# A two-layer decoder trunk: the second feed-forward matrix by seven products, product sums in PSUM, and a new weight ring

## Chip, cores and metric

One core of a Trainium2 chip runs the whole kernel in one launch. The metric is device time in microseconds, from start to end of an execution. The engines are named as in the profile: PE (TensorE, matrix products), DVE (VectorE), ACT (ScalarE), POOL (GpSimd), SP (SyncE, which here issues the DMAs).

## What is computed

Two decoder layers on 512 tokens of width 1024, in float32. Layer 0 mixes tokens by differential and block-sparse attention, layer 1 by gated linear attention; the change does not touch them. After each mixer comes the feed-forward part, which it does touch:

```python
def sqrelu_mlp(x, w1, w2):          # x: 512x1024, w1: 1024x4096, w2: 4096x1024
    return jnp.square(jax.nn.relu(x @ w1)) @ w2

for l in range(DEPTH):              # DEPTH = 2
    ...
    x = layer_norm(DEEPNORM_ALPHA * x + mix, ln_mix_g[l], ln_mix_b[l])
    x = layer_norm(DEEPNORM_ALPHA * x + sqrelu_mlp(x, ffn_w1[l], ffn_w2[l]), ln_ffn_g[l], ln_ffn_b[l])
```

## The kernel before

**Precision by three products.** Each float32 operand is split into a high part in the format fp32r (a copy on ACT) and a low part (a subtraction on DVE); for a weight `parts` does both (L110, L111). A product is then three matmuls into one PSUM bank, high x high, high x low, low x high (`mm3`, L171 to L173).

**Weights** come as units of 512 KB in the order of their use, on SP's queue (L92), into four raw buffers (`rp`). `pump` splits the next unit where the count of units ahead is under a cap; `nxt` takes a unit, `free` gives its buffer back.

**The feed-forward part** (`ffn`) walks through the 4096 hidden features in four blocks of 8 x 128. In a block it first makes hidden features with the first matrix, `pa` banks or pairs, then multiplies them with the block's rows of the second matrix, `pf` banks, and adds the results into `x` (`resid`, L296 and L298).

*First matrix.* A unit is 1024 inputs x 128 hidden features: 8 x 3 = 24 matmuls of 128x512, a plain unit. Two units together can instead go as a pair by the Winograd form of a 2x2 block product, 7 products in place of 8, each of 4 x 3 matmuls of 128x256: 84 matmuls of 256 columns in place of 48 of 512. Its right operands are sums of token quarters, made once per layer (`right_operands`). Its weight sums are made and split by `split_pair` (L135 to L139, then L110 and L111), and `pair` makes the four results out of seven products, each in its own half of a bank `pp`: ACT copies one (p1, L772), DVE adds the rest (L767). Then come relu (L787), square (L712) and the split of the hidden features (L714, L715). Six plain units stand at the head of block 0; the other 26 units of a layer are 13 pairs.

*Second matrix.* Always plain: two halves of 512 output columns, each 8 hidden chunks x 4 token tiles x 3 matmuls of 128x512, so 192 per block, into four banks that DVE adds into `x` after each half.

**Order.** The code names instructions in program order; a scheduler places them on each engine by its own estimates and by urgency marks, so a queue's order is not the text's. Each engine then works strictly in its queue's order.

Of the kernel before, what the change touches and what calls it, by code (L numbers as in the profile page):

```python
# [46 lines left out]
def trunk(ctx, tc, a, out):  # L47
# [34 lines left out]
    NU = wst.shape[0]  # L82
    raws, units, late = {}, {}, {}
    W = {"dma": 0, "split": 0, "used": 0, "slots": 0, "cap": 6}
    pairs = {u + 16 * b + j for u in FFN_UNITS for b in range(FF // P // FBLK) for j in range(0 if b else NPLAIN, FBLK, 2)}

    def dma_unit():
        for fn in late.pop(W["dma"], ()):
            fn()
        if W["dma"] < NU:  # L90
            r = rp.tile([P, 1024], F32, tag="raw", name="raw")
            nc.sync.dma_start(r, wst[W["dma"]])  # L92
            raws[W["dma"]] = r
            W["dma"] += 1

    def pop_raw():
        u = W["split"]
        while W["dma"] <= u:
            dma_unit()
        W["split"] += 1  # L100
        return raws.pop(u)

    def ahead():
        while W["dma"] < min(W["split"] + 4, NU):
            dma_unit()

    def parts(w, i, src):

        n = src.shape[-1] // 512
        A.activation(w[:, 0, i:i + n, :], src.rearrange("p (n c) -> p n c", n=n), AF.Copy)  # L110
        V.tensor_tensor(w[:, 1, i:i + n, :], src.rearrange("p (n c) -> p n c", n=n), w[:, 0, i:i + n, :].bitcast(F32),  # L111
                        op=ALU.subtract)
# [1084 lines left out]
```

## Time and profile before

| | before |
|---|---|
| time, median of 3 runs | 1173.81 us (1173.73 to 1173.92) |
| profiled execution, its own time | 1172.42 us |
| its span (first to last instruction) | 1170.6 us |
| PE busy | 1155.2 us, 99 % of the span |
| DVE busy | 793.0 us, 68 % |
| ACT busy | 548.1 us, 47 % |
| first layer's feed-forward part | about 254.8 to 597.5 us |
| second layer's feed-forward part | about 832 to 1164.5 us |

An engine's busy time is the union of its instructions' durations, so a PE whose matmuls overlap can be busy all the time; what a matmul costs is read from the distance of two starts. Idle time in brackets stands before the row's first instruction, with what ended it.

### The profile page before, as it was taken

What the parts mean: (1) busy time and instruction counts of PE and PEld (TensorE: products, weight loads), DVE (VectorE), ACT (ScalarE), POOL (GpSimd) and SP (SyncE); (2) the same over time, 40 slices, a digit from 0 to 9 for tenths busy, and PEclk for the clock granted to TensorE, in tenths of its full rate; (3) what the DMA queues carried; (4) which work ended last, traced back from release to release, by engine and by line L of the source; (5) the groups of instructions that cost most, each with busy time, mean ns of one, the idle gap of its engine ahead of it and who ended that gap; (6) DMA issues with size and microseconds to landing.
All of it is one profiled execution on the core that took longest, in us unless ns stands there. A gap on an engine that the chain in (4) does not pass through costs nothing.

```text
span 1170.6 us, 16693 instructions
## 1 busy us (share of the span) xinstructions
PE 1155.2 (99%) x6682; PEld 1008.9 (86%) x6682; DVE 793.0 (68%) x1299; ACT 548.1 (47%) x890; POOL 48.4 (4%) x64
## 2 busy tenths in 40 slices
PE   9999999999999999999999999999999999999997
PEld 6788877898899899899888888888988998988986
DVE  6788673679468477487547656587784874865946
ACT  5745375547237146156236433643471551642631
POOL 1122300000000000000110000000000000000000
PEclk9999999999999999999999999999999999999999
DMA  9622050023226125127123122501051251251421
GB/s 319 232 72 73 8 161 32 19 73 118 99 60 191 38 73 180 54 67 252 37 68 108 55 72 73 180 19 57 34 181 54 70 165 55 87 165 36 121 78 73
DMA packets 34094, 114.33 MB, mean 98 GB/s; under 512 B 4192, under 2 KB 5216, under 8 KB 34016
## 3 DMA queue, kind: packets, MB, share of 16 engines
q1 hardware_dynamic: 32368, 108.22, 28.6%
q0 software_dynamic: 1648, 5.05, 1.4%
q8 instruction: 52, 0.85, 0.3%
q14 instruction: 26, 0.21, 0.1%
HBM read 111.15 MB, written 2.10 MB: 97 GB/s over the span
## 4 chain that ended last, share of the span: by engine, by line
PE 93%; issue 2%; ACT 2%; DVE 1%; DMA 0%; POOL 0%; DVEq 0%; ACTq 0%; POOLq 0%
PE pf L171 11%; PE pf L172 11%; PE pf L173 11%; PE pp L173 7%; PE pp L172 7%; PE pp L171 7%; PE pa L171 5%; PE pa L173 5%; PE pa L172 5%; PE pb L171 3%; PE pb L172 3%; PE pb L173 3%; PE pl L1000 2%; PE sc L521 1%; PE pv L171 1%
## 5 line engine op out<-in xcount | busy, mean ns | idle before, releaser
L111 DVE TENSOR_TENSOR w<-raw,w 128x1024 fp32r<-128x1024 f32 (+1 forms) x190 | 222.2, 1179 | 57.2 <-ACT w L110 56.3
L110 ACT ACTIVATE w<-raw 128x1024 fp32r<-128x1024 f32 (+1 forms) x190 | 188.2, 997 | 92.2 <-DMA raw<-in_wst 19.9
L171 PE MATMUL pf<-w,hh 128*128 128x512 f32 x504 | 196.4, 390 | 0.0
L172 PE MATMUL pf<-w,hh 128*128 128x512 f32 x504 | 196.2, 389 | 0.0
L173 PE MATMUL pf<-w,hl 128*128 128x512 f32 x504 | 196.1, 389 | 0.0
L110 ACT ACTIVATE w<-sf 128x1024 fp32r<-128x1024 f32 x52 | 55.0, 1058 | 215.6 <-PE pf L173 138.7
L172 PE MATMUL pp<-xTl,w 128*128 128x256 f32 x416 | 117.7, 283 | 0.0
L173 PE MATMUL pp<-xTh,w 128*128 128x256 f32 x416 | 117.7, 283 | 0.0
L171 PE MATMUL pp<-xTh,w 128*128 128x256 f32 x416 | 117.7, 283 | 0.0
L173 PEld LDWEIGHTS pf<-w,hl 128*128 128x128 f32 x504 | 94.6, 188 | 19.8
L171 PEld LDWEIGHTS pf<-w,hh 128*128 128x128 f32 x504 | 94.6, 188 | 19.5
L172 PEld LDWEIGHTS pf<-w,hh 128*128 128x128 f32 x504 | 94.6, 188 | 19.1
L171 PE MATMUL pa<-xTh,w 128*128 128x512 f32 x264 | 106.0, 403 | 0.0
L173 PE MATMUL pa<-xTh,w 128*128 128x512 f32 x264 | 103.1, 391 | 0.0
L172 PE MATMUL pa<-xTl,w 128*128 128x512 f32 x264 | 102.9, 390 | 0.0
L111 DVE TENSOR_TENSOR w<-sf,w 128x1024 fp32r<-128x1024 f32 x52 | 63.6, 1224 | 56.5 <-ACT w L110 56.5
L171 PE MATMUL pp<-T,w 128*128 128x256 f32 x312 | 88.3, 283 | 0.0
L172 PE MATMUL pp<-T,w 128*128 128x256 f32 x312 | 88.3, 283 | 0.0
L173 PE MATMUL pp<-T,w 128*128 128x256 f32 x312 | 88.3, 283 | 0.0
L171 PEld LDWEIGHTS pp<-xTh,w 128*128 128x128 f32 x416 | 79.8, 192 | 0.3
L172 PEld LDWEIGHTS pp<-xTl,w 128*128 128x128 f32 x416 | 79.8, 192 | 0.3
L173 PEld LDWEIGHTS pp<-xTh,w 128*128 128x128 f32 x416 | 79.8, 192 | 0.0
(260 smaller groups left out, 2264.2 us busy)
## 6 DMA issues: line engine op xcount, KB each, us to landing
raw<-in_wst SPq DMA_DIRECT2D x190, 512.0 KB, 3.8
xraw<-in_xT SPq DMA_DIRECT2D x8, 256.0 KB, 5.1
x<-in_x SPq DMA_DIRECT2D x4, 512.0 KB, 6.9
gb<-in_lng POOLq DMA_DIRECT2D x4, 512.0 KB, 5.7
gb<-in_lnb POOLq DMA_DIRECT2D x4, 512.0 KB, 7.5
out_x<-x SPq DMA_DIRECT2D x7, 256.0 KB, 2.0
tab<-in_rope SPq DMA_DIRECT2D x2, 512.0 KB, 5.9
raw<-in_wst SPq DMA_DIRECT2D x4, 128.0 KB, 4.4
```

The lines of the kernel that those rows point to most:

```text
L110: A.activation(w[:, 0, i:i + n, :], src.rearrange("p (n c) -> p n c", n=n), AF.Copy)
L111: V.tensor_tensor(w[:, 1, i:i + n, :], src.rearrange("p (n c) -> p n c", n=n), w[:, 0, i:i + n, :].bitcast(F32), op=ALU.subtract)
L171: PE.matmul(o, l[0], r[0], start=first, stop=False)
L172: PE.matmul(o, l[0], r[1], start=False, stop=False)
L173: PE.matmul(o, l[1], r[0], start=False, stop=last)
L521: PE.matmul(ps[:, :n], q, k, start=i == 0, stop=False)
L1000: PE.matmul(pl[:, h * P:(h + 1) * P], z, z, start=True, stop=True)
```

## The change

- **Second matrix.** In blocks 0, 1 and 2 of each layer `second` makes the product by 7 products of half size, each 2 x 2 x 2 x 3 = 24 matmuls of 128x512. Left operands are sums of hidden-feature quarters (`s1`, the in-place sums of `a21` and `a12`, then the split by `left` into tiles `ho`); right operands are sums of weight quarters made in place in four tiles `w2` (`add_block`, L230) and split into the ring. Products that enter one result in sequence accumulate in one pair of banks, and are added into `x` after each step: 14 residual adds in place of 8. Block 3 stays plain.
- **First matrix.** `PLAIN = (6, 4, 4, 0)` plain units by block: 1, 2, 2 and 4 pairs, 9 per layer for 13. In `pair` four products accumulate in the bank `ba` and two in `bc`; ACT copies their content in between (p1 L878, u2 L886; p5 L882), DVE's adds read it (L805).
- **Weights.** The ring `qp` has 7 half buffers of 1024 values per partition. A plain unit or an entry of the second matrix takes 2, an entry of a pair 2 or 1 (7 for the whole pair). A plain unit can also take a whole buffer of pool `u`, up to `W["un"]`, which is 0 in the feed-forward part but for its end. Three raw buffers in place of four; pools are opened anew by stage.

The core of the diff; in the new kernel line numbers are other ones, and L117 is the low part of any split, L116 its high part, L867 a pair's matmul, L394 and L396 residual adds.

```diff
-NPLAIN = 6
+NB = FF // P // FBLK
+PLAIN = (6, 4, 4, 0)
+NQ = 7
...
-    rp = ctx.enter_context(tc.tile_pool(name="rp", bufs=4))
+    rp = ctx.enter_context(tc.tile_pool(name="rp", bufs=3))
+    qp = ctx.enter_context(tc.tile_pool(name="qp", bufs=NQ))
...
+    def room(kind):
+        if kind == "unit":
+            return W["q"] + 2 <= NQ or W["u"] < W["un"]
+        return W["q"] + kind <= NQ
+
+    def take(kind):
+
+        if kind == "unit" and W["q"] + 2 > NQ:
+            W["u"] += 1
+            w = t8("w", (P, 2, 1024), F32R)
+            return ("u", 1), w[:, 0], w[:, 1]
+        n = 1 if kind == 1 else 2
+        W["q"] += n
+        if n == 1:
+            w = q4()
+            return ("q", 1), w[:, :512], w[:, 512:]
+        return ("q", 2), q4(), q4()
+
...
+        steps = ((0, 0, None), (0, 0, lambda a, b_, c, d: sub(a, b_, a)), (0, 0, lambda a, b_, c, d: sub(a, d, a)),
+                 (1, 0, None), (0, 1, lambda a, b_, c, d: sub(b_, d, b_)), (1, 1, None),
+                 (1, 0, lambda a, b_, c, d: sub(c, c, a)))
+        return [entry(i, n, half, pre, m == 6) for m, (i, n, pre) in enumerate(steps) for half in range(2)]
...
+        def pair(p, right):
+
+            ba, bb, bc = (bank("pp")[:, :256] for _ in range(3))
...
+            p1, p5, u2 = t1("p1"), t1("p5"), t1("u2")
+            c11, c12, c21, c22 = H[0][:, 0, p, :], H[0][:, 1, p, :], H[1][:, 0, p, :], H[1][:, 1, p, :]
+            w = nxt()
+            prod(ba, w, 0, "b11", True)
+            A.activation(p1, ba, AF.Copy)
+            v = nxt()
+            prod(bc, v, 0, "t1", True)
+            done(v)
+            A.activation(p5, bc, AF.Copy)
+            v = nxt()
+            prod(ba, v, 0, "t2", False)
+            done(v)
+            A.activation(u2, ba, AF.Copy)
+            prod(bb, w, 1, "b21", True)
+            done(w)
+            add(c11, p1, bb)
+            w = nxt()
+            prod(ba, w, 0, "t3", False)
+            add(c22, p5, ba)
+            v = nxt()
+            prod(bc, v, 0, "b22", False)
+            done(v)
+            add(c12, u2, bc)
+            prod(ba, w, 1, "t4", False)
+            done(w)
+            r = H[0][:, :, p, :]
+            A.activation(r, r, AF.Relu)
+            square(0, p)
+            A.activation(c22, c22, AF.Relu)
+            A.activation(c21, ba, AF.Relu)
+            square(1, p)
+
...
+        def second():
+
+            c = {k: [bank("pf") for _ in range(2)] for k in "AC"}
+            a11, a21, a12, a22 = H[0][:, 0], H[0][:, 1], H[1][:, 0], H[1][:, 1]
+
+            def left(src, halves=False):
+                h, l = (t4("ho", (P, 4, 256), F32R) for _ in range(2))
+                for z in ((slice(0, 2), slice(2, 4)) if halves else (slice(0, 4),)):
+                    split(h[:, z], l[:, z], src[:, z])
+                return h, l
+
+            def prod(k, op, first):
+                for half in range(2):
+                    w = nxt()
+                    r = [z.rearrange("p (j c) -> p j c", j=2) for z in w[1:]]
+                    for j in range(2):
+                        for tt in range(2):
+                            l = [z[:, 2 * half + j, tt * P:(tt + 1) * P] for z in op]
+                            for n, (x_, y_) in enumerate(((0, 0), (0, 1), (1, 0))):
+                                PE.matmul(c[k][tt], l[x_], r[y_][:, j, :], start=first and half == j == n == 0,
+                                          stop=half == j == 1 and n == 2, skip_group_check=True)
+                    release(w[0])
+                    pump(2)
+
+            o11 = left(a11, True)
+            s = t4("s1", (P, 4, 256))
+            add(s, a21, a22)
+            o1 = left(s)
+            prod("A", o11, True)
+            into_x(0, 0, c["A"])
+            sub(s, s, a11)
+            o2 = left(s)
+            prod("C", o1, True)
+            into_x(1, 1, c["C"])
+            o12 = left(a12)
+            sub(a21, a11, a21)
+            prod("A", o2, False)
+            into_x(0, 1, c["A"])
+            o3 = left(a21)
+            sub(a12, a12, s)
+            c["B"] = [bank("pf") for _ in range(2)]
+            prod("B", o12, True)
+            into_x(0, 0, c["B"])
+            o4 = left(a12)
+            prod("A", o3, False)
+            into_x(1, 1, c["A"])
+            o22 = left(a22)
+            prod("C", o4, False)
+            into_x(0, 1, c["C"])
+            prod("A", o22, False)
+            into_x(1, 0, c["A"])
+
...
+            if not fin:
+                second()
+                continue
```

Three places in the order of the instructions.

DVE in block 1 of layer 0, where the second matrix begins; before, from the last pair's hidden split on (`sf` are sums for pairs of the next block, `hl` the hidden features' low part, `pf` the product's banks):

```order
L715 TENSOR_TENSOR hl_3575<-r_3459,hh_3574 128x512 [waits DVE_49,Activation_49]
L111 TENSOR_TENSOR w_3725<-raw_3562,w_3725 128x1024 [waits DMAHW6_49,Activation_49]
L135 TENSOR_TENSOR sf_3729<-raw_3609 128x512 [waits DMAHW7_49,PE_49]
L138 TENSOR_TENSOR sf_3729<-raw_3562,raw_3609 128x512
L136 TENSOR_TENSOR sf_3729<-sf_3729,raw_3562 128x512 [waits DVE_49]
L139 TENSOR_TENSOR sf_3729<-raw_3562,sf_3729 128x512 [waits DVE_49]
L111 TENSOR_TENSOR w_3726<-sf_3729,w_3726 128x1024 [waits Activation_49]
L296 TENSOR_TENSOR x_112<-x_112,pf_3578 128x512 [waits PE_49]
L296 TENSOR_TENSOR x_112<-x_112,pf_3579 128x512 [waits PE_49]
L296 TENSOR_TENSOR x_112<-x_112,pf_3580 128x512 [waits PE_49]
```

after, from the last sum of the last pair on (`w2` weight tiles, `w` ring entries, `s1` and `ho` sums and splits of hidden features):

```order
L805 TENSOR_TENSOR hb_3101<-u2_3374,pp_3371 128x256 [waits PE_49]
L230 TENSOR_TENSOR w2_3169<-w2_3291,w2_3169 128x2x512 [waits DMAHW6_49,DMAHW0_49]
L117 TENSOR_TENSOR w_3487<-w2_3169,w_3486 128x1024 [waits PE_49,Activation_49]
L805 TENSOR_TENSOR s1_3506<-hb_3101,hb_3102 128x1024 [waits DVE_49,Activation_49]
L117 TENSOR_TENSOR ho_3501<-hb_3101,ho_3500 128x512 [waits Activation_49]
L117 TENSOR_TENSOR w_3525<-w2_3414,w_3524 128x1024 [waits PE_49,Activation_49]
L117 TENSOR_TENSOR ho_3509<-s1_3506,ho_3508 128x1024 [waits Activation_49]
L230 TENSOR_TENSOR w2_3169<-w2_3291,w2_3169 128x2x512
L394 TENSOR_TENSOR x_115<-x_115,pf_3496 128x512 [waits PE_49]
L394 TENSOR_TENSOR x_115<-x_115,pf_3497 128x512 [waits PE_49]
L117 TENSOR_TENSOR w_3542<-w2_3169,w_3541 128x1024 [waits Activation_49]
L806 TENSOR_TENSOR s1_3506<-s1_3506,hb_3101 128x1024
```

Between the last pair and the end of the second matrix, sums and splits of this very matrix and of its left operands now stand in the row with the residual adds; before, it was work for the block after.

ACT around the start of a pair (`p1`, `p5`, `u2` are copies out of the pair's banks `pp`, `r` and `hb` hidden features); before, the second pair of block 1:

```order
L712 ACTIVATE r_3049<-r_3049 128x512 [waits Activation_49]
L712 ACTIVATE r_3050<-r_3050 128x512 [waits Activation_49]
L714 ACTIVATE hh_3165<-r_3049 128x512 [waits Activation_49]
L110 ACTIVATE w_3211<-raw_2964 128x512 [waits DMAHW3_49,DVE_49]
L714 ACTIVATE hh_3171<-r_3050 128x512 [waits Activation_49]
L110 ACTIVATE w_3341<-raw_3092 128x1024 [waits DMAHW4_49,PE_49]
L772 ACTIVATE p1_3179<-pp_3175 128x256 [waits PE_49]
L110 ACTIVATE w_3342<-sf_3345 128x1024 [waits DVE_49,PE_49]
L787 ACTIVATE r_3182<-r_3182 128x512 [waits DVE_49]
```

after, the second pair of block 1:

```order
L116 ACTIVATE w_3312<-s_3308 128x512 [waits DVE_49,PE_49]
L116 ACTIVATE w_3355<-raw_3167 128x1024 [waits DMAHW5_49,PE_49,Activation_49]
L900 ACTIVATE hb_3101<-hb_3101 128x2x256 [waits DVE_49]
L116 ACTIVATE w_3360<-raw_3134 128x512 [waits DVE_49,PE_49]
L816 ACTIVATE hb_3101<-hb_3101 128x2x256 [waits Activation_49]
L903 ACTIVATE hb_3102<-pp_3234 128x256
L878 ACTIVATE p1_3372<-pp_3369 128x256 [waits PE_49]
L816 ACTIVATE hb_3102<-hb_3102 128x2x256 [waits Activation_49]
L882 ACTIVATE p5_3373<-pp_3371 128x256 [waits PE_49]
L116 ACTIVATE w_3420<-w2_3169 128x1024 [waits DMAHW7_49]
L886 ACTIVATE u2_3374<-pp_3369 128x256 [waits PE_49]
```

Three copies out of the banks of the pair stand where there was one, each between splits and activations, and the two of them from `pp_3369` now stand between products that go on in that bank.

DVE at the start of the kernel (`p0` is the first projection, which the rotary step reads; `w` the split of the weights after it); before:

```order
L242 TENSOR_TENSOR xTl_91<-xraw_93,xTh_90 128x512 [waits DMAHW4_49,Activation_49]
L242 TENSOR_TENSOR xTl_91<-xraw_93,xTh_90 128x512 [waits DMAHW5_49,Activation_49]
L111 TENSOR_TENSOR w_243<-raw_244,w_243 128x1024 [waits DMAHW7_49,Activation_49]
L111 TENSOR_TENSOR w_260<-raw_248,w_260 128x1024 [waits DMAHW0_49,Activation_49]
L273 CAST identb_128<-ident_113 128x128 [waits DMAHW1_49]
L274 TENSOR_SCALAR subg_115<-subg_115 128x1 [waits DMAHW2_49]
L111 TENSOR_TENSOR w_265<-raw_254,w_265 128x1024 [waits DMAHW4_49,Activation_49]
L111 TENSOR_TENSOR w_270<-raw_256,w_270 128x1024 [waits DMAHW5_49,Activation_49]
L423 STREAM_SHUFFLE rt_214<-p0_132 128x512 [waits PE_49]
```

after:

```order
L340 TENSOR_TENSOR xTl_94<-xraw_96,xTh_93 128x512 [waits DMAHW4_49,Activation_49]
L340 TENSOR_TENSOR xTl_94<-xraw_96,xTh_93 128x512 [waits DMAHW5_49,Activation_49]
L521 STREAM_SHUFFLE rt_219<-p0_137 128x512 [waits PE_49]
L526 SCALAR_TENSOR_TENSOR rot_218<-p0_137,tab_97 128x512 [waits DMAHW6_49]
L527 SCALAR_TENSOR_TENSOR rt_219<-rt_219,tab_97 128x512 [waits DVE_49]
L117 TENSOR_TENSOR w_251<-raw_248,w_250 128x1024 [waits DMAHW7_49,Activation_49]
L117 TENSOR_TENSOR w_265<-raw_254,w_264 128x1024 [waits DMAHW0_49,Activation_49]
L542 TENSOR_TENSOR q2_226<-rot_218,q2_224 64x512 [waits Activation_49]
L543 TENSOR_TENSOR q2_227<-rot_218,q2_225 64x512 [waits Activation_49]
```

The shuffle and two rotary multiplies moved ahead of the splits of the first whole units.

## Rows read from the trace of the kernel before

**Rows 1.** Page, busy time by engine; page, the last chain by engine.

```profile
PE 1155.2 (99%) x6682; PEld 1008.9 (86%) x6682; DVE 793.0 (68%) x1299; ACT 548.1 (47%) x890; POOL 48.4 (4%) x64
...
PE 93%; issue 2%; ACT 2%; DVE 1%; DMA 0%; POOL 0%; DVEq 0%; ACTq 0%; POOLq 0%
```

**Rows 2.** Busy time by stretch: length, engines (instructions), granted clock, DMA share, GB/s.

```profile
290.40:333.90 43.50, 43.50 (x194) 36.04 (x194) 22.38 (x29) 11.24 (x16) 0.00 (x0) 1.00 0.28 92
333.90:376.00 42.10, 42.10 (x345) 41.73 (x344) 37.19 (x57) 28.36 (x42) 0.00 (x0) 1.00 0.45 139
...
254.80:597.50 342.70, 342.66 (x2108) 309.34 (x2108) 238.37 (x354) 155.78 (x227) 11.84 (x25) 1.00 0.32 101
```

**Rows 3.** Timeline of PE, second matrix: start, duration, engine, line, operation, tiles, shapes.

```profile
299.78 0.39 PE L172 MATMUL pf<-w,hh 128*128 128x512 f32 x1
...
300.91 0.39 PE L171 MATMUL pf<-w,hh 128*128 128x512 f32 x1
```

**Rows 4.** Timeline of PE inside a pair of block 0; 23 rows between.

```profile
282.80 0.28 PE L171 MATMUL pp<-T,w 128*128 128x256 f32 x1
...
285.68 0.28 PE L171 MATMUL pp<-xTh,w 128*128 128x256 f32 x1
```

**Rows 5.** Timeline of DVE, block 0: a pair, then the second matrix.

```profile
277.86 1.22 DVE L111 TENSOR_TENSOR w<-sf,w 128x1024 fp32r<-128x1024 f32 x1
279.00 1.22 DVE L730 TENSOR_TENSOR xTl<-tf,xTh 128x1024 fp32r<-128x1024 f32 x1
280.13 1.22 DVE L111 TENSOR_TENSOR w<-sf,w 128x1024 fp32r<-128x1024 f32 x1
281.27 4.09 DVE L111 TENSOR_TENSOR w<-raw,w 128x512 fp32r<-128x512 f32 x4
...
285.88 0.41 DVE L767 TENSOR_TENSOR u<-p,pp 128x256 f32<-128x256 f32 x1
286.21 0.41 DVE L767 TENSOR_TENSOR r<-p,pp 128x256 f32<-128x256 f32 x1
...
301.11 0.69 DVE L135 TENSOR_TENSOR sf<-raw 128x512 f32<-128x512 f32 x1 [2.41 <-PE pf L173]
301.72 0.68 DVE L138 TENSOR_TENSOR sf<-raw 128x512 f32<-128x512 f32 x1
302.32 0.68 DVE L136 TENSOR_TENSOR sf<-sf,raw 128x512 f32<-128x512 f32 x1
...
307.64 1.23 DVE L111 TENSOR_TENSOR w<-sf,w 128x1024 fp32r<-128x1024 f32 x1 [3.91 <-ACT w L110]
```

**Rows 6.** Timeline of ACT in the same pair.

```profile
281.51 1.05 ACT L110 ACTIVATE w<-raw 128x1024 fp32r<-128x1024 f32 x1
282.46 0.62 ACT L712 ACTIVATE r<-r 128x512 f32<-128x512 f32 x1
```

**Rows 7.** Groups by line and shape: busy us, mean ns of one, idle before.

```profile
L712 ACT ACTIVATE r<-r 128x512 f32<-128x512 f32 x64 | 37.0, 617 | 0.2
...
L772 ACT ACTIVATE p<-pp 128x256 f32<-128x256 f32 x26 | 9.6, 370 | 2.3 <-PE pp L173 2.3
```

**Rows 8.** Timelines of DVE and of PE at the start of the kernel.

```profile
17.04 2.54 DVE L111 TENSOR_TENSOR w<-raw,w 128x1024 fp32r<-128x1024 f32 x2 [2.35 <-ACT w L110]
...
22.36 0.74 DVE L423 STREAM_SHUFFLE rt<-p 128x512 f32<-128x512 f32 x1
23.00 0.67 DVE L428 SCALAR_TENSOR_TENSOR rot<-p,tab 128x512 f32<-128x512 f32 x1
23.59 0.68 DVE L429 SCALAR_TENSOR_TENSOR rt<-rt,tab 128x512 f32<-128x512 f32 x1
...
17.16 0.39 PE L173 MATMUL p<-xTh,w 128*128 128x512 f32 x1
...
18.06 0.39 PE L171 MATMUL pb<-w,xTh 128*128 128x512 f32 x1
```

**Rows 9.** Page, DMA issues (KB each, median us to landing); timeline of PE.

```profile
raw<-in_wst SPq DMA_DIRECT2D x190, 512.0 KB, 3.8
...
57.53 0.30 PE L528 MATMUL pt<-ident,e 128*128 128x128 f32 x1 [2.14 <-ACT k L454]
```

More of the change, by code (lines that the diff above doesn't have):

```diff
@@ L81, in trunk @@
     wst = a["wst"]
[L82 to L112, printed above, removed]
@@ L146, in pump, with load_to @@
-    def pump():
-        n = 4 if W["split"] in pairs else 1
-        if W["split"] < NU and W["slots"] + n <= W["cap"]:
-            split_unit()
-    def nxt():
-        u = W["used"]
-        while W["split"] <= u:
-            split_unit()
-        W["used"] += 2 if u in pairs else 1
-        return units.pop(u)
+    late = {}
+    loads, entries = [], []
+    W = {"load": 0, "ready": 0, "q": 0, "u": 0, "un": 3, "ahead": 3}
+    got, ops, held = {}, deque(), deque()
+    def load_to(n):
+        while W["load"] < min(n, len(loads)):
+            for fn in late.pop(W["load"], ()):
+                fn()
+            loads[W["load"]]()
+            W["load"] += 1
@@ new lines, in ready, with pump @@
+    def ready():
+        need, kind, fn = entries[W["ready"]]
+        load_to(need)
+        W["ready"] += 1
+        c, h, l = take(kind)
+        fn(h, l)
+        ops.append((c, h, l))
+        load_to(need + W["ahead"])
+    def pump(n=1):
+        while n and W["ready"] < len(entries) and room(entries[W["ready"]][1]):
+            ready()
+            n -= 1
+    def nxt():
+        if not ops:
+            ready()
+        c, h, l = ops.popleft()
+        held.append(c)
+        return c, h, l
@@ new lines, in add_units, with add_pair, first, s1 @@
+    def add_units(u0, n):
+        for u in range(u0, u0 + n):
+            k = add_load(raw(u), wst[u])
+            entries.append((k, "unit", lambda h, l, u=u: split(h, l, got.pop(u))))
+    def add_pair(u):
+        add_load(raw(u), wst[u])
+        k, st = add_load(raw(u + 1), wst[u + 1]), {}
+        sub = lambda o, p, q: V.tensor_tensor(o, p, q, op=ALU.subtract)
+        def first(h, l):
+            split(h, l, got[u])
+        def s1(h, l):
+            a2, st["s"] = got[u + 1], t2("s")
+            V.tensor_tensor(st["s"], a2[:, :512], a2[:, 512:], op=ALU.add)
+            split(h, l, st["s"])
+        def s2(h, l):
+            sub(st["s"], st["s"], got[u][:, :512])
+            split(h, l, st["s"])
+        def s3(h, l):
+            a1, a2 = got[u], got.pop(u + 1)
+            sub(a2[:, :512], a1[:, :512], a2[:, :512])
+            split(h, l, a2)
+        def s4(h, l):
+            a12 = got.pop(u)[:, 512:]
+            sub(a12, a12, st.pop("s"))
+            split(h, l, a12)
+        return [(k, 2, first), (k, 1, s1), (k, 1, s2), (k, 2, s3), (k, 1, s4)]
@@ new lines, in add_ffn, with wa @@
+    def add_ffn(u, layer):
+        for b in range(NB):
+            add_units(u, PLAIN[b])
+            first, second = [], []
+            for j in range(PLAIN[b], FBLK, 2):
+                first += add_pair(u + j)
+            if b < NB - 1:
+                second = add_block(u + FBLK, layer, b)
+            entries.extend(first + second)
+            if b == NB - 1:
+                add_units(u + FBLK, FBLK)
+            u += 2 * FBLK
+    def wa(op):
+        h, l = (z.rearrange("p (k c) -> p k c", k=KT) for z in op[1:])
+        return lambda k: (h[:, k, :], l[:, k, :])
```

276 lines of the change are left out of this document (143 added, 133 removed).

## The prediction, made before the changed kernel ran

> **What bounds the kernel now.** I read the busy shares first, then the chain that ended last, and there is only one candidate: TensorE is busy 99 % of the span and 93 % of the last chain is its own matmuls [rows 1]. [...] So a matmul taken out is worth its full slot, as long as DVE and ACT deliver operands in time. [...]
>
> **Prices.** A matmul's duration in the table (0.39 us) is pipelined and is no cost; the slot is the distance of starts. In the second matrix's stage 300.91 - 299.78 = 1.13 us hold five, 0.226 each [rows 3], and 43.5 us for its 192 give 0.2266, which I use. In a pair 24 products of 128x256 lie between 282.80 and 285.68: 0.120 each [rows 4]. DVE back to back: 128x1024 at 277.86, 279.00, 280.13, 281.27, so 1.14; 128x512 at 301.11, 301.72, 302.32, so 0.605; an add from PSUM of 128x256 at 285.88 and 286.21, so 0.33 [rows 5]. ACT: 128x1024 0.95 (281.51 to 282.46) [rows 6]; a 128x256 copy out of PSUM lasts 0.370 [rows 7].
>
> **PE work.** In each layer blocks 0, 1 and 2 take 168 matmuls of 128x512 in the second matrix in place of 192: 6 x 24 x 0.2266 = -32.6 us in all. In return the first matrix has 9 pairs per layer where it had 13 (1, 2, 2, 4 by block), so 8 pairs go back to plain units. A pair is 84 x 0.120 = 10.08 us, its plain form 48 x 0.2266 = 10.88; each return costs 0.80, together +6.4. Sum: **-26.2 us**, if PE never waits more than now.
>
> [...]
>
> **The second matrix's stage on DVE.** For each of the three blocks `second` and `add_block` need 14 splits of weight sums, 8 weight sums in place (L230), 7 splits of hidden operands, 4 hidden sums, each 128x1024, and 14 residual adds of 128x512. That is 33 x 1.14 + 14 x 0.605 = 46.1 us of DVE against 168 x 0.2266 = 38.1 us of PE. Before, the same stage had idle gaps of 2.4 and 3.9 us on DVE [rows 5]. So it depends on how much of the 46 us is done before the stage begins. The ring decides that: 7 half buffers, 2 for each entry of this matrix, hence three entries ahead. The order of the changed kernel shows it for block 1 (first place in the section on the change): three of the splits stand ahead of `s1`, and from `s1` to the last split there are 39 DVE rows, 26 of 128x1024 and 13 of 128x512: 26 x 1.14 + 13 x 0.605 = 37.5 us. `s1` cannot begin before the last pair's results are relu'd and squared on ACT, about 1.6 us after its last product (one 256-column and two 512-column activations, 0.37 + 2 x 0.617 [rows 7]), and after the last split 10 matmuls (2.3) remain. 1.6 + 37.5 + 2.3 = 41.4 for 38.1 of PE work: **3.3 us lost**, without a single DVE wait counted. Block 2 has the same rows, but behind its last split DVE waits in order on residual adds that need PE's last product, with the next pair's sums and splits queued behind: 4.8 + 0.3. Block 0 is worst: four splits (two of them of the second matrix, 4.0 us by the price above with their 512-column company) stand between the adds for c11 and c22 of its only pair, so the pair stalls 0.5, both left operands come late (0.85, 0.35 and 1.5), and later entries again (1.0, 1.2, 0.9): 6.1 to 6.3.
>
> **Inside the pairs.** Four products now accumulate in one bank; between them ACT copies p1 and u2 out of it and DVE's add for c22 reads it, and PE may not go on in that bank until each is done; before, every product had its own half bank and nobody waited. The scheduler fills in other products (second place). ACT serves in order: `w_3355` waits for a ring buffer that the last product of the pair before gives back, and p1 of the next pair is queued behind it, with relu and square. I put this at 0.5 us per block for blocks 1 and 2, and 0.5 for the three transitions of block 3, where the ring entry comes earlier. The bounds: nothing, if the other product always covers it, and about 1.9 us a pair, if three copies stood bare, each at 0.62 (0.37 [rows 7], a tail of 0.16 after the slot, two handovers of some 0.05). I take the low end, since a product of 12 x 0.12 = 1.44 us lies between in most places.
>
> Per layer: 3.3 + 5.1 + 6.2 + 1.0 + 0.5 = 16.1, for both **+32.2 us**. Layer 1 has the same order of rows.
>
> **The start.** Three raw buffers in place of four. Now DVE begins the first split at 17.04, the moment ACT has made the high part, and PE goes over to `pb` at 18.06 without a stall to speak of [rows 8]. After, DVE's shuffle and rotary multiplies of `p0` stand ahead of that split (third place): they take 2.0 us now (22.36 to 24.3 [rows 8]) and can begin when `p0`'s first product ends, 17.55, so the low part comes at about 20.7, while PE has four matmuls (0.9) to do without it: 1.75 lost. The load of the next raw must now wait for that split, and lands 3.8 us or more after its issue [rows 9], split at about 26, where PE wants it at 24.8: about 1.1. **+2.8**, from 0 (PE has a gap of 2.1 us before 57.53 anyway, behind ACT [rows 9], and could lose less there) to 5. For the other changed stages, whose ring holds as much as before, +0.7.
>
> **Sum.** The profiled run took 1172.42 us, 1.4 below the median of 1173.81. 1172.4 - 26.2 + 32.2 + 2.8 + 0.7 = 1181.9; on the median's footing **1183 us**, 0.8 % slower.
>
> **Rivals.**
> *The DVE excess is hidden* (faster). The 4 plain units and 2 pairs ahead of block 1's second stage leave DVE half idle: 4 x 24 x 0.2266 + 2 x 10.08 = 41.9 us of PE, 4 x 1.14 + 2 x (2 x 1.14 + 7 x 0.605 + 3 x 0.33) = 19.6 of DVE. If scheduler and ring let DVE get further ahead than the three entries I read, or the waits I chained overlap, each stage loses under 1 us: 1173.8 - 26.2 + 6 + 3.5 = 1157, and 1148 if nothing is lost at all. The gain is 13.1 us per layer and the 3.5 us of start and other stages take 1.75 of it: a loss below 11.3 per layer, where I have 16.1, makes the kernel faster. Against it: 39 rows in order with no room for more in the ring. For it: I added late operands one by one, and a stall early in a block gives DVE time for the next. 0.28 with the partial case (about 1165).
> *Gain and loss cancel*: losses of 10.2 to 12.5 per layer beside the same 3.5 us, 1171.5 to 1176.1. 0.13.
> *The pairs stall at each copy*: 1.3 us more in each of 18 pairs, +24, so 1207. For it speaks that ACT's queue holds 0.95 us splits ahead of each copy [rows 6]; against it that another product lies between. 0.12. [...]
> *The change does not do what it says* is out: the order has 3402 matmuls of 512 columns for 3162 and 2052 of 256 for 2724, which is -6 x 24 + 8 x 48 and -8 x 84.
>
> **How the numbers follow.** The forecast (1176 to 1194 with its own errors: losses of 14 per layer with no loss at the start, 1176.3, to 20 with 5, 1193.3) has 0.47. Range: 1160 to 1200, which leaves out the case of nearly everything hidden (about 0.1) and that of copies stalling (about 0.1). This kernel's measurement can tell 0.2 %, 2.3 us, from no change. Faster 0.28, same 0.13, slower 0.59.
>
> **What would show it.** Right: in the three second stages of each layer PE has gaps, released by DVE (a split, L117) or by ACT behind one; DVE is busy over 90 % there, and each lasts 41 to 45 us in place of 43.5. PE's gaps over both layers sum to some 30 us. Pairs take 10.1 to 10.7. At the start PE waits about 1.7 us at 19 for a split queued behind the shuffle. Wrong: second stages of 38 to 39 us (the first rival), or pairs of 11.5 or more with gaps released by ACT's copies (the third).

## The result, and the profile after

The changed kernel takes 1205.52 us (median of 4 runs, 1204.55 to 1206.36) beside 1173.77 (1173.37 to 1173.92) of the kernel before: **2.7 % slower, ratio 1.0271 with an interval of 1.0253 to 1.0289**. The forecast was 1183, with a range to 1200: the sign is right, the size is not. The profiled execution took 1205.73 us, its span is 1204.0.

The page after, busy time by engine and the last chain by engine, as in [rows 1]:

```profile
PE 1161.2 (96%) x6250; PEld 973.4 (81%) x6250; DVE 874.0 (73%) x1311; ACT 598.2 (50%) x974; POOL 47.0 (4%) x64
...
PE 68%; DVE 19%; ACT 6%; issue 4%; DMA 1%; POOL 1%; DVEq 0%; ACTq 0%; POOLq 0%
```

DVE has 19 % of the chain where it had 1 %. Cut at the first matmul of each feed-forward part and of gated linear attention (`pf<-xTh`; a feed-forward part then begins some 10 us ahead of the stretch in [rows 2]), the span divides so:

| part | before | forecast | after |
|---|---|---|---|
| start, attention, its output | 244.9 | 247.7 | 254.8 |
| first feed-forward part | 342.8 | 345.8 | 352.1 |
| gated linear attention | 234.3 | 234.3 | 241.7 |
| second feed-forward part | 348.6 | 351.6 | 355.3 |

(The forecast's 0.7 for other stages is not in it.) Within the first feed-forward part, cut where the first product of a stage starts (its first 10.4 us, the same in both kernels, are left out):

| stage | before | forecast | after | e1, no sums | e9, four raws |
|---|---|---|---|---|---|
| block 0, first matrix | 34.7 | 35.2 | 36.5 | 36.6 | 36.5 |
| block 0, second | 43.5 | 43.8 | 43.3 | 40.7 | 43.3 |
| block 1, first | 40.3 | 42.4 | 41.9 | 41.8 | 41.6 |
| block 1, second | 43.5 | 41.4 | 42.3 | 39.7 | 42.2 |
| block 2, first | 40.3 | 42.4 | 42.4 | 42.1 | 41.8 |
| block 2, second | 43.5 | 43.2 | 42.1 | 41.3 | 42.3 |
| block 3, first | 40.3 | 40.8 | 43.8 | 41.6 | 40.0 |
| block 3, second, and norm | 46.2 | 46.2 | 49.4 | 49.6 | 50.0 |

Busy time of three second stages and of block 3's pairs, the view of [rows 2] (length, PE, PEld, DVE, ACT, POOL, granted clock, DMA share, GB/s):

```profile
301.70:345.00 43.30, 40.78 (x169) 30.84 (x169) 43.27 (x45) 23.19 (x26) 0.00 (x0) 1.00 0.01 2
386.90:429.20 42.30, 40.79 (x171) 31.08 (x169) 42.27 (x44) 22.52 (x25) 0.00 (x0) 1.00 0.02 2
471.60:513.70 42.10, 40.07 (x168) 30.52 (x167) 42.07 (x45) 20.44 (x23) 0.00 (x0) 1.00 0.00 0
513.70:557.50 43.80, 41.76 (x338) 40.38 (x337) 35.70 (x54) 29.87 (x55) 1.05 (x2) 1.00 0.39 135
```

In the second stages DVE is busy to the last 0.03 us, where before it was busy 22.4 of 43.5 in block 0's [rows 2]. The timelines of DVE and PE in block 0 show how it binds: DVE's rows follow each other 1.13 to 1.14 apart with no idle bracket, and PE waits for the low part of `ho`:

```profile
306.68 1.21 DVE L117 TENSOR_TENSOR w<-w,w 128x1024 fp32r<-128x1024 f32 x1
307.82 1.21 DVE L230 TENSOR_TENSOR w<-w,w 128x1024 f32<-128x1024 f32 x1
308.95 1.21 DVE L117 TENSOR_TENSOR ho<-s,ho 128x1024 fp32r<-128x1024 f32 x1
...
310.22 0.98 PE L932 MATMUL pf<-w,ho 128*128 128x512 f32 x3 [1.11 <-DVE ho L117]
```

That much was foreseen. Five things were not, each with its rows. In block 3's pairs ACT waits for a raw weight, and PE for what hangs on it and, in three of the four, for the copy p1:

```profile
528.07 0.50 PE L867 MATMUL pp<-T,w 128*128 128x256 f32 x2 [0.21 <-ACT p L878]
...
553.31 1.06 ACT L116 ACTIVATE w<-raw 128x1024 fp32r<-128x1024 f32 x1 [1.84 <-DMA raw<-in_wst]
...
556.02 0.51 PE L867 MATMUL pp<-T,w 128*128 128x256 f32 x2 [1.28 <-DVE hb L805]
```

At the end of the first feed-forward part three weight splits of the next stage stand between the steps of the layer norm's reciprocal root, and PE waits for the normalised tile:

```profile
600.85 1.22 DVE L117 TENSOR_TENSOR w<-raw,w 128x1024 fp32r<-128x1024 f32 x1
601.99 0.15 DVE L406 TENSOR_TENSOR y<-y,v 128x1 f32<-128x1 f32 x1
602.06 1.22 DVE L117 TENSOR_TENSOR w<-raw,w 128x1024 fp32r<-128x1024 f32 x1
603.19 0.15 DVE L407 TENSOR_SCALAR y<-y 128x1 f32<-128x1 f32 x1
603.25 1.21 DVE L117 TENSOR_TENSOR w<-raw,w 128x1024 fp32r<-128x1024 f32 x1
...
605.86 1.42 PE L433 MATMUL pt<-ident,x 128*128 128x128 f32 x8 [2.29 <-DVE x L425]
```

The mixers show the same picture: a split ahead of the state `S` and of the probabilities `e`:

```profile
784.36 1.21 DVE L117 TENSOR_TENSOR w<-raw,w 128x1024 fp32r<-128x1024 f32 x1
785.49 0.16 DVE L407 TENSOR_SCALAR y<-y 128x4 f32<-128x4 f32 x1
785.56 0.47 DVE L1231 SCALAR_TENSOR_TENSOR S<-S,dec,ds 128x256 f32<-128x256 f32 x1
...
786.09 0.70 PE L1227 MATMUL ds<-gv,khT 128*128 128x256 f32 x2 [1.32 <-DVE S L1231]
...
87.98 1.22 DVE L117 TENSOR_TENSOR w<-raw,w 128x1024 fp32r<-128x1024 f32 x1
...
91.47 0.33 PE L629 MATMUL pt<-ident,e 128*128 128x128 f32 x1 [0.93 <-DVE e L669]
```

Matmuls that wait for nothing start farther apart: six in 1.56 us, so (1.56 - 0.39) / 5 = 0.234 each where [rows 3] had 0.226:

```profile
317.82 1.56 PE L932 MATMUL pf<-w,ho 128*128 128x512 f32 x6
```

And TensorE's granted clock, 1.00 almost throughout (0.994 in the mean, 0.998 before), was at a lower level, 0.50, for three stretches, each after PE had waited (2.18 us before 183.02; 2.29 before 605.86; 1.32 and 0.91 in 784 to 788). The view of [rows 2], and two matmuls of 256 columns that start 0.21 apart where 0.12 is usual:

```profile
183.70:187.10 3.40, 3.35 (x13) 2.94 (x14) 0.46 (x2) 3.07 (x7) 0.00 (x0) 0.50 0.62 175
607.00:610.30 3.30, 3.30 (x18) 3.30 (x17) 2.87 (x9) 2.38 (x6) 1.23 (x4) 0.50 0.78 259
787.90:791.20 3.30, 3.30 (x13) 2.55 (x12) 3.30 (x16) 1.40 (x3) 0.00 (x0) 0.50 0.68 236
...
607.51 0.42 PE L272 MATMUL pf<-xTh,w 128*128 128x256 f32 x1
607.72 0.42 PE L270 MATMUL pf<-xTh,w 128*128 128x256 f32 x1
```

By estimate from the 0.50 and from these starts each stretch costs up to half its length, 1.7 us, so up to 5 of the 33.3 us between the two profiled executions. That of the kernel before has no such stretch ahead of its last 6 us, though PE waits 2.14 us (before 57.53) and 2.18 us (before 175.75) there too.

### The profile page after: what moved, and what is told of

It reads as the page before. It is cut to its first block, busy times and chain, and to the rows that moved or that the text cites. A ratio compares the mean times of both kernels' runs of the same rounds, so it can differ in the third digit from the quotient of the medians.

```text
span 1204.0 us, 15900 instructions
## 1 busy us (share of the span) xinstructions
PE 1161.2 (96%) x6250; PEld 973.4 (81%) x6250; DVE 874.0 (73%) x1311; ACT 598.2 (50%) x974; POOL 47.0 (4%) x64
## 4 chain that ended last, share of the span: by engine, by line
PE 68%; DVE 19%; ACT 6%; issue 4%; DMA 1%; POOL 1%; DVEq 0%; ACTq 0%; POOLq 0%
DVE w L117 7%; PE pf L932 7%; PE pa L270 7%; PE pa L272 7%; PE pa L271 7%; PE pp L867 6%; PE pf L271 4%; PE pf L270 4%; PE pf L272 4%; PE pb L271 4%; PE pb L270 4%; PE pb L272 4%; DVE ho L117 2%; ACT w L116 2%; DVE w L230 2%
## 5 line engine op out<-in xcount | busy, mean ns | idle before, releaser
L117 DVE TENSOR_TENSOR w<-raw,w 128x1024 fp32r<-128x1024 f32 (+2 forms) x166 | 188.6, 1149 | 129.4 <-PE pa L271 38.7
L932 PE MATMUL pf<-w,ho 128*128 128x512 f32 x1008 | 246.6, 400 | 11.9 <-DVE ho L117 7.9
L932 PEld LDWEIGHTS pf<-w,ho 128*128 128x128 f32 x1008 | 185.2, 188 | 67.9 <-DVE ho L117 13.6
L116 ACT ACTIVATE w<-raw 128x1024 fp32r<-128x1024 f32 (+2 forms) x166 | 162.7, 987 | 88.2 <-DMA raw<-in_wst 46.8
L270 PE MATMUL pa<-xTh,w 128*128 128x512 f32 x392 | 156.9, 400 | 0.5
L272 PE MATMUL pa<-xTh,w 128*128 128x512 f32 x392 | 153.6, 392 | 0.0
L867 PE MATMUL pp<-T,w 128*128 128x256 f32 x864 | 114.7, 283 | 5.3 <-DVE hb L805 2.8
L116 ACT ACTIVATE w<-w 128x1024 fp32r<-128x1024 f32 x84 | 86.8, 1054 | 65.1 <-DVE w L230 53.0
L867 PEld LDWEIGHTS pp<-T,w 128*128 128x128 f32 x864 | 106.7, 189 | 9.3 <-DVE hb L805 4.1
L117 DVE TENSOR_TENSOR w<-w,w 128x1024 fp32r<-128x1024 f32 x84 | 101.1, 1217 | 8.8 <-ACT w L116 8.6
L867 PE MATMUL pp<-xTh,w 128*128 128x256 f32 x432 | 87.0, 282 | 0.3
L270 PEld LDWEIGHTS pa<-xTh,w 128*128 128x128 f32 x392 | 74.0, 189 | 16.4 <-ACT w L116 2.3
L272 PEld LDWEIGHTS pa<-xTh,w 128*128 128x128 f32 x392 | 73.6, 188 | 16.0
L271 PE MATMUL pb<-w,xTh 128*128 128x512 f32 x192 | 75.9, 396 | 2.7 <-DVE w L117 2.7
L270 PE MATMUL pb<-w,xTh 128*128 128x512 f32 x192 | 76.8, 403 | 0.9 <-ACT w L116 0.9
L867 PEld LDWEIGHTS pp<-xTh,w 128*128 128x128 f32 x432 | 70.7, 189 | 1.5 <-ACT w L116 1.1
L867 PE MATMUL pp<-xTl,w 128*128 128x256 f32 x216 | 61.0, 282 | 0.0
L116 ACT ACTIVATE ho<-hb 128x1024 fp32r<-128x1024 f32 (+1 forms) x36 | 32.7, 910 | 39.4 <-DVE hb L806 39.2
```

Source lines behind the costliest of these rows:

```text
L116: A.activation(h, src, AF.Copy)
L117: V.tensor_tensor(l, src, h.bitcast(F32), op=ALU.subtract)
L270: PE.matmul(o, l[0], r[0], start=first, stop=False)
L271: PE.matmul(o, l[0], r[1], start=False, stop=False)
L272: PE.matmul(o, l[1], r[0], start=False, stop=last)
L867: PE.matmul(o, w[x_], z[y_], start=first and k == n == 0, stop=k == 3 and n == 2, skip_group_check=True)
```

## Experiments

Each ratio is to the kernel before on the same chip (1173.0 to 1173.3 us there), with its 95 % interval. "Less" and "more" are to the kernel that the run changes, unless another is named. In the diffs `...` stands for lines that are not shown.

### The second stage: VectorE's queue

**e1**, in `entry`:

```diff
-                if pre:
+                if False:
```

> The changed kernel without the eight in-place weight sums (L230) in each of the six second stages that go by seven products; it leaves that part of the computation out. Theory A (the second stage is bound by VectorE's queue): 8 x 1.14 = 9.1 us of DVE less per stage, 46.1 - 9.1 = 37.0 us against 38.1 of PE, so the five us a stage loses fall to about one: six stages give back 20 to 27 us, 1179 to 1186. Rival B (the stage waits on something else: ring buffers, copies out of PSUM, DMA): less than 5 us, above 1200.

1186.68 us (1.0113, 1.0098 to 1.0129), 18.8 less. The six stages fell from 42.1 to 43.3 to 39.7 to 41.3, block 1's to the PE's own pace:

```profile
384.50:424.20 39.70, 39.66 (x170) 31.35 (x169) 36.13 (x38) 22.45 (x25) 0.00 (x0) 1.00 0.06 16
```

DVE's queue binds the second stage (theory A), but the six stages give back only about 12 of the 18.8 us, not 20 to 27: PE's own pace takes over, 39.7 / 168 = 0.236 a matmul and not 0.2266. Some 5 us come from block 3's pairs of both layers (41.6 for 43.8 in the first), still with three raw buffers, so part of their loss seems to be DVE's queue running late behind block 2's second stage. The other 1.7 lies in gated linear attention.

**e2**, in `add_block`:

```diff
-        sub = lambda o, p, q: V.tensor_tensor(o, p, q, op=ALU.subtract)
+        sub = lambda o, p, q: G.tensor_tensor(o, p, q, op=ALU.subtract)
```

> The changed kernel with the same weight sums (L230) on GpSimd in place of VectorE. The kernel before has a 128x512 sum of two tensors on GpSimd at 1.34 us, so 2.7 for 128x1024, 21 us per stage of about 41, off DVE's queue. Theory A, if GpSimd leaves DVE's rate alone: 1180 to 1190. If the two slow each other, or GpSimd's sums come late for the first entries: 1195 or more. Rival B: no change, about 1205.

1259.03 us (1.0732, 1.0714 to 1.0750): 53.5 more. By groups and on DVE's timeline:

```profile
L230 POOL TENSOR_TENSOR w<-w,w 128x1024 f32<-128x1024 f32 x36 | 108.9, 3029 | 74.7 <-DVE w L117 70.1 <-issue 3.6
...
313.47 3.39 DVE L117 TENSOR_TENSOR w<-w,w 128x1024 fp32r<-128x1024 f32 x1
```

A DVE split that took 1.21 us as changed takes 3.39 here, and the mean of its group (L117, `w<-w,w`) went from 1.22 to 1.66: the sums moved to GpSimd were not simply taken off DVE, whose other instructions got longer. Part of the 53.5 may be the clock's: over the whole profiled run the granted clock was 0.974 (0.994 as changed), and 0.90 over 300:350, where PE was busy 40.4 of 50 us. No run parts the two, and none shows why the instructions got longer.

**e3**: all blocks take the plain branch (`second()` is not called, hidden splits in every block, plain units in the ring):

```diff
...
-            if b < NB - 1:
-                second = add_block(u + FBLK, layer, b)
-            entries.extend(first + second)
-            if b == NB - 1:
-                add_units(u + FBLK, FBLK)
+            entries.extend(first)
+            add_units(u + FBLK, FBLK)
...
```

> The changed kernel with the second matrix plain in all blocks (192 matmuls each); pairs, PSUM sums, ring and the share of pairs as changed. PE gets 32.6 us more. Theory A: the second stages lose some 15 us per layer now, so 30 come back and the kernel stays near 1208 (1203 to 1213): the seven products of the second matrix are worth nothing net, and what remains slower than before, some 34 us, lies in the pairs given back (6.4), the ring, the raw buffers and the order in the other stages. Rival B (the loss lies outside the second stages): 1230 to 1238.

1219.13 us (1.0389, 1.0373 to 1.0404). So the seven products earn 13.6 us of the 32.6 they take off PE, more than theory A's near nothing and less than the rival's 25 to 32. The plain stages took 47.4, 44.8 and 44.8 us, not 43.5, with no wait in blocks 1 and 2 and DVE busy 15.5: again a slower pace, 44.8 / 192 = 0.233 a matmul.

```profile
392.30:437.10 44.80, 44.80 (x194) 36.05 (x193) 15.54 (x17) 11.08 (x14) 0.00 (x0) 1.00 0.34 105
```

### Pairs and raw buffers

**e4**:

```diff
-PLAIN = (6, 4, 4, 0)
+PLAIN = (6, 0, 0, 0)
```

> The changed kernel with 13 pairs per layer again (plain units 6, 0, 0, 0). PE gets 6.4 us less. If a pair costs its 10.08 us and little more: 1199 to 1201. If each further pair loses what the pairs of block 3 lose in the trace of the changed kernel (3.2 us for four, most of it a wait for a raw weight): 8 x 0.8 = 6.4 lost again, 1204 to 1207.

1202.05 us (1.0245, 1.0229 to 1.0260): 3.5 less, between the two. Four pairs in blocks 1 and 2 took 42.0, as long as two pairs and four plain units.

**e9** (the 32 bytes are e5's, below):

```diff
-    rp = ctx.enter_context(tc.tile_pool(name="rp", bufs=3))
+    rp = ctx.enter_context(tc.tile_pool(name="rp", bufs=4))
...
-    new_stage(u=8, t=25)
+    new_stage(u=8, t=23)
...
-    W = {..., "ahead": 3}
+    W = {..., "ahead": 4}
...
-        new_stage(u=10, h=5, t=4, p=6)
+        new_stage(u=10, h=5, t=2, p=6)
...
```

> The changed kernel with the 32 bytes and four raw buffers (four loads ahead), the number of units ahead left as changed. Theory E (three raw buffers cost, wherever weights are split often): the four pairs of block 3 take 40.1 us in place of 43.8 in both layers, the start and the mixers get some 5 us back: 1200.8 - 7.4 - 5 = 1188, 1185 to 1192. Rival (raws matter in the pairs alone): 1193 to 1195. Raws of no effect: 1200.

1191.45 us (1.0154, 1.0138 to 1.0169), 9.4 less than e5. Block 3's pairs take 40.0 and 40.1 us in the two layers, without the waits for raws:

```profile
512.60:552.60 40.00, 39.83 (x336) 39.24 (x334) 34.67 (x53) 30.16 (x56) 1.05 (x2) 1.00 0.40 145
```

That is below the 40.3 of before, but the copies between products in one bank are not free: with the 32 bytes a pair's matmuls start 0.115 to 0.119 apart, which makes 39.1 for the four, so 0.9 us of short waits remain, the two longest (0.24 us) ended by the copy p1. Gated linear attention fell from e5's 241.5 to 237.0, of which by estimate, at half of a stretch's length, some 2.6 are the clock's: it was at the lower level for two stretches there in e5 (606.1 to 609.3 and 787.0 to 790.2), in e9 for the end of one; over the whole runs the mean was 0.994 and 0.996. The attention part did not move (254.2, 254.5).

**e10**, the kernel before:

```diff
-    rp = ctx.enter_context(tc.tile_pool(name="rp", bufs=4))
+    rp = ctx.enter_context(tc.tile_pool(name="rp", bufs=3))
...
-        while W["dma"] < min(W["split"] + 4, NU):
+        while W["dma"] < min(W["split"] + 3, NU):
```

> The kernel before with three raw buffers and three loads ahead in place of four, nothing else. Theory E: its thirteen pairs per layer each need two raws, and lose what block 3's pairs lose in the changed kernel, 0.9 each, 26 x 0.9 = 23 us, and the mixers some 5: 1195 to 1205. Rival (the raw wait comes from the new split by entries, not from the count): 1173 to 1177.

1179.77 us (1.0053, 1.0034 to 1.0072), 6.5 more. In the profiled execution all of it is in the attention part (252.3 for 244.9): PE's idle time there rose by 3.9 us, and after waits of 3.35 and 2.67 us the clock was 0.50 in 62.30:65.60 and in 181.80:185.10 (0.996 over the whole run, 0.998 before), up to 1.7 us each by estimate. Every pair stage stayed at 40.3, so theory E as I put it falls: three raws alone do no harm to the old pairs. What makes them scarce in the changed kernel is consistent with `s3` and `s4`, which write their sums into the raw buffers and so hold both until their splits; before, sums went to a tile of their own. That a split holds its raws while it waits for room in the ring would fit as well. No run undid either by itself.

**e11**: e9 with e4's line.

> As the run with four raws and 32 bytes, with 13 pairs per layer. Theory E: without raw waits the pairs of blocks 1 and 2 take 40.3 for four in place of 41.9 for two and four plain units, 4 x 1.6 = 6.4 us less than that run: 1180 to 1184. Rival (VectorE's queue then starts the second matrix later, and eats it): no less than that run.

1184.48 us (1.0091, 1.0072 to 1.0110), 7.0 less than e9: with four raws the pairs given back are pure loss, and four pairs take 39.9 and 40.2. Theory E holds for the changed kernel's pairs.

### Units ahead, and scratch tiles

**e6**, allowed whole units by stage:

```diff
-    W["un"] = 4
+    W["un"] = 5
...
-        W["un"] = 5
+        W["un"] = 6
...
-            W["un"] = 2
+            W["un"] = 4
...
-    W["un"] = 5
+    W["un"] = 7
```

> The changed kernel with more whole units allowed ahead beside the ring, as many in all as the kernel before had: 5 and 6 in the attention stages (4 and 5), 4 at the end of a feed-forward part (2), 7 in the last part of gated linear attention (5). Theory D (the 16 us lost outside the feed-forward parts and 5 at their end come from splits that stand late in DVE's and ACT's queues because fewer units may be ahead): 1190 to 1198. Rival (the order there is the scheduler's in any case, or the three raw buffers set it): 1203 to 1207.

1209.27 us (1.0311, 1.0290 to 1.0331): 3.8 more, 245.9 in gated linear attention, where PE now waits 4.07 us for `wgs` (before 633.28) and the clock was 0.50 in 632.30:639.00 (0.992 over the whole run). Without that wait and the low clock 1202 to 1204 us would be left by estimate, not 1190 to 1198: theory D falls.

**e8**: e5, e6 and four raws together.

> The changed kernel with the 32 bytes, the greater number ahead and four raw buffers with four loads ahead (two tiles less in pool t and in the small pool for it). If the three are what was lost outside the second stages: about 1205.5 - 4 (address) - 11 (ahead) - 6 (start 1.8, block 3 2 x 1.5, some of the attention) = 1184, 1180 to 1189. If the second stages' DVE queue is all of it: above 1195.

1196.36 us (1.0199, 1.0177 to 1.0221). Without e6's part (e9) it is 4.9 faster, about what the same wait of 4.07 us for `wgs` costs here too: the count was no mend.

**e13**: e9, and in `ln_a`

```diff
-        zs = [t2("z") for _ in cs]
+        zz = t4("z") if "h" in pool else None
+        zs = [zz[:, c] if zz is not None else t2("z") for c in cs]
```

> As the run with 32 bytes and four raws, and the layer norm's scratch (two tiles per token tile) from the pool of 4 KB tiles in place of the small pool, which holds two tiles there. Theory F (the end of the first feed-forward part takes 50.0 us in place of 46.2 for want of scratch tiles): 46 to 47.5, 1191.5 - 3 = 1188.5. Rival (three weight splits stand in DVE's queue in the middle of the norm): 49 to 50, 1191.

1190.04 us (1.0153, 1.0138 to 1.0168). The end took 49.3 for 50.0, and a mean clock of 1.00 there for 0.98 (552.60:602.50 in e9) is enough for that: theory F falls, and the rival, splits in DVE's queue, stays. No run took the splits away. That the second layer's end, with no next weights to split, lost only 0.3 (52.2 for 51.9) speaks for it too.

### Where the operands begin

**e5** and **e12**, unused bytes ahead of the pools that are opened by stage (e12 with 24 in place of 8):

```diff
+    padp = ctx.enter_context(tc.tile_pool(name="padp", bufs=1))
+    padp.tile([P, 8], F32, name="pad")
     psp = ctx.enter_context(tc.tile_pool(name="psp", bufs=8, space=bass.MemoryType.PSUM))
```

> The changed kernel with 32 unused bytes per partition ahead of the pools that are opened by stage, and nothing else. In the trace of the changed kernel the matmuls of the second matrix (left operands ho and hs in these pools) start 0.231, 0.231, 0.238 us apart, in before 0.2267; in the program these tiles begin 32 bytes off a multiple of 64 per partition, in before on one. Theory C (the address costs the 7 ns): 0.2267 again in all of them. Block 3's second matrix (2 x 192 matmuls) gives 2.5 us back, the six other second stages (168 x 0.007 = 1.2 each) little where DVE sets their end: 1198 to 1203 in all. Rival (the layout of the tile or the ring's): 0.233 still, 1205.

1200.83 us (1.0237, 1.0212 to 1.0262), 4.7 less: the time lies in theory C's range, but the products with `ho` start 0.2295 apart, not 0.2267.

> The changed kernel with 96 unused bytes in place of 32, so that the stage's tiles, the ring and the transposed input all begin at the same place within 128 bytes, as in before. Theory C2 (what counts is whether the two operands of a matmul begin at the same place): 0.2267 in all matmuls of 512 columns (0.2334 as changed, 0.2295 with 32 bytes), 0.120 in those of 256 with T (0.118 and 0.115). The time: within 3 us of 1200.8 (the one gains what the other loses, and six of eight second stages are bound by VectorE). Rival (being on a multiple of 64 is what counts): the same starts as with 32 bytes.

1202.47 us (1.0244, 1.0223 to 1.0265). Seven matmuls in 1.75 us, (1.75 - 0.39) / 6 = 0.227:

```profile
317.82 1.75 PE L934 MATMUL pf<-w,ho 128*128 128x512 f32 x7
```

and 0.120 in the pairs, as C2 had it. The rival falls: by the program these tiles begin on a multiple of 64 in e5 as well, and the starts differ. With both operands alike within 128 bytes the two shapes went opposite ways: 512 columns started closest (0.227, for 0.2295 in e5 and 0.234 as changed), 256 columns with T farthest apart (0.120, for 0.115 in e5).

**e7**, e5's two lines ahead of pool `up` in the kernel before.

> The kernel before with the same 32 unused bytes put ahead of its pools of weights and operands, so that these tiles begin 32 bytes off a multiple of 64. Theory C: here TensorE is the bound throughout, so all of it shows: 7 ns for each of the 3162 matmuls of 512 columns is 22 us, and for the 2724 of 256 columns between nothing and 19: 1185 to 1215. Rival (address has no effect): 1173 to 1174.

1177.15 us (1.0033, 1.0022 to 1.0043). Theory C's 22 us was far too much, since weights and hidden features moved together: 0.227 between those two, 0.233 where a shifted weight meets the unshifted input, 0.118 in the pairs. The mixers lost 2.3 and 3.8, the feed-forward parts gained 1.1 each.

**e14 to e18**, the kernel before: tiles of `up` enlarged, weights of pairs 64 bytes further in (e14 without), in e16 to e18 also those of the first three units. e14 to e16 have 2080 elements and 24 small tiles, e17 2176 and 22, e18 2112 and 23:

```diff
-    def t8(name, shape=(P, NH, T), dt=F32):
-        return up.tile(list(shape), dt, tag="u", name=name)
+    def t8(name, shape=(P, NH, T), dt=F32, at=0):
+        z = up.tile([P, 2176], dt, tag="u", name=name)[:, at:at + math.prod(shape[1:])]
+        ...
...
-        w = wtile()
+        w = wtile(16 if u in (32, 33, 34, 128, 129, 130) else 0)
...
-        ta, tb, tc_, td = (wtile() for _ in range(4))
+        ta, tb, tc_, td = (wtile(16) for _ in range(4))
```

> Control for the next two: the kernel before with tiles of 8320 bytes in place of 8192 in its pool of weights, and one tile less (24) in the pool of small tiles. All tiles still begin at the same place within 128 bytes. 1173 (1171 to 1176), matmuls at 0.2267 and 0.120; more if the missing tile makes waits.

1180.65 us (1.0074, 1.0059 to 1.0089): a control that was none. The second matrix's stage took 44.3 us for 43.5 without a wait, 44.3 / 192 = 0.231 a matmul, with tiles that begin alike within 128 bytes here too.

> That control with the weights of the 26 pairs begun 64 bytes further in their tile, so that in a pair's matmuls the two operands begin 64 bytes apart. By C2 as the earlier runs show it (0.115 with T 64 bytes apart, 0.120 at the same place): 2184 matmuls x 0.0046 = 10 us, all on a path that TensorE sets: 1163 (1160 to 1167). If DVE, at 9.9 of 10.1 us per pair, becomes the bound in the pairs: 1167 to 1172. Rival (no effect here): 1173.

> As the run before it, and the first three units of each feed-forward part too, whose 144 matmuls each layer x 2 of 256 columns then have operands 64 bytes apart: 288 + 144 of them x 0.0046 = 2 us less than that run: 1161.

1175.22 (1.0019, 1.0009 to 1.0029) and 1174.42 us (1.0011, 1.0001 to 1.0022), 5.4 and 6.2 less than e14. The pairs pay, about half of what I expected.

> The kernel before with the weights of pairs and of the first three units 64 bytes further in their tiles, as in the run before, but with tiles of 8704 bytes (three small tiles less, 22), so that all tiles begin at the same place within 512 bytes, as in before. The control with 8320 showed 0.231 for the second matrix's matmuls, so the same place within 128 bytes does not do. Theory C3 (512 does): 0.2267 in the second matrix and the mixers, 0.1165 in the pairs: four pairs 39.2 us in place of 40.3, 1173 - 2 x 3.6 - 1.5 = 1164 (1162 to 1167). Rival (another distance counts, or 22 tiles make waits): 1170 or more.

> The same with tiles of 8448 bytes and 23 small tiles: the same place within 256 bytes, not within 512. If 256 is what counts: 1164 as the run before it; if 512: 0.231 in half of the second matrix's matmuls, 1170.

**1166.31 us (0.9940, 0.9926 to 0.9954)** and 1167.53 us (0.9948, 0.9934 to 0.9962): both beat either kernel. The second stage of e17 is back at 43.5, its four pairs take 39.6:

```profile
289.10:332.60 43.50, 43.50 (x194) 36.04 (x193) 22.86 (x30) 11.96 (x15) 0.00 (x0) 1.00 0.31 98
332.60:372.20 39.60, 39.60 (x337) 39.56 (x337) 34.70 (x53) 26.64 (x39) 0.00 (x0) 1.00 0.42 132
```

e18, with tiles alike within 256 bytes and not within 512, has the same 0.227 and 0.118.

## Why the prediction was right or wrong

**PE work, -26.2: right in count.** 3402 and 2052 matmuls by form. The price was not constant: the second matrix's went from 0.2267 to 0.233 with its left operands 32 bytes off, and was 0.227 when 96 bytes had moved them on (e12). I had taken the slot of a matmul as a property of its shape.

**The second stages: right.** Forecast 43.8, 41.4 and 43.2 us, measured 43.3, 42.3 and 42.1, sum 127.7 for 128.4; e1 shows the mechanism. The order read row by row was good for it. Some luck is in the figures: PE's slower pace (168 x 0.007 = 1.2 us a stage) hardly shows because DVE sets the end. PE's waits beyond a slot add up to some 34 us in the two feed-forward parts, near the 30 named as a sign.

**Pairs and PSUM: the low end was right.** 40.0 us for four with four raws. The measured 1205.5 lies beside the third rival's 1207 by chance: its waits at copies are there, but the six that show as idle time (0.4 us each, in block 3's pairs) come to 2.6 us in all, not 24.

**Block 3's pairs, 0.5 per layer: mis-sized.** 3.5 and 3.8, so 10.9 us a pair, outside the 10.1 to 10.7 named as a sign. I had counted three raws only at the start of the kernel and never priced the wait for a raw inside a pair. e9 takes it back. Block 0's pair lost 1.8 where I had 0.5: PE waits there for splits (0.6 us before 292.0, 0.4 before 297.15, both ended by ACT's `w` L116).

**"For the other changed stages, whose ring holds as much as before, +0.7": the step that failed.** The term came from no row. The mixers and the start lost 17.3 us in the profiled run, where I had 3.5, and the end of the first feed-forward part 3.2, where I had none. The premise was wrong as well: ring and whole units together had room for 7 units, not 8, and for 8, not 9 or 10. But e6 shows that this count is not the reason. What is shown: 4.5 of gated linear attention's 7.4 come back with the fourth raw (e9), the clock's part among them; some 2 us go with the place of operands (e12; 3.8 for the larger shift in e7); and the splits in the middle of other chains stand in the rows above. Most of the attention part's 9.9 can be added up from the trace: PE's idle time went from 6.7 to 11.5 us, the low clock after 183.70 cost up to 1.7, and the 512-column matmuls into `pb` and `pa` start 2 ns farther apart (0.231 for 0.229 in the mean), some 1.5 us over 700. I had walked DVE's order in the feed-forward part alone and taken the rest as unchanged because its code is.

**The start, +2.8: right in mechanism, short in size.** PE waited 1.71, 0.74, 1.06 and 0.72 us beyond a matmul's slot between 20 and 29 us: 4.2, within my 0 to 5. The first two were the split behind the shuffle, and the gap at 57 (now at 61) shrank from 2.3 to 1.5.

```profile
20.33 0.50 PE L271 MATMUL pb<-w,xTh 128*128 128x512 f32 x1 [1.55 <-DVE w L117]
```

**What stays open**: what undoes the attention part's 9.9 us. e10 shows that three raws cost the old kernel 7.4 there, the clock's part included, yet the fourth raw gave the new one nothing back; two waits at 91 and 122 us (1.1 and 1.7) are splits and rotary steps ahead of `e`, and why the scheduler put them there was not tried. Nor was why some waits of PE were followed by a clock of 0.50 (2.18 us before 183.02 and 2.29 before 605.86, as changed) and others, as long, were not (2.14 and 2.18 in the kernel before); no run was made for it.

## What to carry to other kernels

This kernel's main engine was busy 99 % and hardly waited, and the start and the mixers, whose code the change leaves alone, lost 17.3 us: a change of buffers or order has to be walked through every stage that uses them, not only where the arithmetic changes. A product form that saves matmuls must be priced on the engine that makes its sums, and here that bill was right to 1 us a layer for the second stages. Before comparing two layouts, note where the tiles of matmul operands begin: moving a pool by 32 bytes changed the time by 4 to 5 us either way (e5, e7). And look at the granted clock by stretch: behind a wait of 2.29 us it was 0.50 for 3.3 us here, by estimate up to 1.7 us on top of the wait.
